# Zero products ahead of the first matmuls, and two of four modulation blocks multiplied in fp32 as they land

## The chip, the cores and the metric

The kernel runs on one core of one Trainium2 chip. The metric is the device time of one execution in microseconds. Three runs of the kernel before took 1945.74, 1946.46 and 1949.13 us (median 1946.46). TensorE multiplies (PE in the profile, its weight loads PEld), VectorE (DVE), ScalarE (ACT) and GpSimd (POOL) work on rows and columns, SyncE (SP) issues most DMAs.

## The reference

One layer of a diffusion backbone over 1024 latent and 256 context tokens of width 1024. What matters here is its start: a conditioning vector gives shift and scale of the first normalisation, and every projection reads the modulated tokens.

```
mod = (silu(cond) @ w_ada + b_ada)              # cond: two rows, c and c_ctx; w_ada: 1024 x 6144
sh1, sc1, gt1, sh2, sc2, gt2 = split(mod, 6)    # 1024 columns each
u = rmsnorm(x, g_norm1) * (1 + sc1) + sh1
proj = u @ w_in                                 # pooling, gating, q, k, v, output gate, branch gates
...                                             # three branches, merge, w_out, second norm, feed-forward
```

All inputs and outputs are fp32.

## The kernel before, in words

Tokens are in ten row tiles of 128 x 1024 (`xt[0]` to `xt[9]`; the first eight are latent). They are worked on in three groups of 512, 512 and 256 tokens. The projections need u transposed: per group g and k-tile k (128 of the 1024 columns), `tr(k, g)` (L251) makes up to four 128x128 transposes into one PSUM buffer (`pt_u` in the trace), and `mc(k, g)` (L255, through `modulate_cols`, L176) has ACT apply scale `a1` and shift `sh1` per column (`val_u`), stores the fp32 result to DRAM for later (`scr_u`, a POOL DMA), and has DVE split it into a rounded part and a rest (`u0h`, `u0l` and so on).

The number format matters. `F32R` is a reduced fp32 that PE multiplies in one pass. A product at nearly fp32 accuracy is made from three F32R products: high x high, high x low, low x high (`dense`, L117 to L125, three products of 128x512 for a k-tile of group 0). Weights are split the same way by `load_w` (L89): ACT copies to `hi`, DVE subtracts to `lo`.

Shift and scale come from the first 2048 columns of w_ada, in four blocks of 512 columns: blocks 0 and 1 are the two halves of the shift, 2 and 3 the two halves of the scale. Each block is eight landed tiles `ada[b, k]` of 128x512 fp32 (256 KB each, `wa` in the trace; L195 to L200 issue them on SP in the order 0, 2, weight k0, 1, 3). `mod_split(b, ks)` (L221) does, for each k-tile of a block:

- an ACT copy of the landed tile to F32R (`wah`) and a DVE subtract for the rest (`wal`);
- on PE, a product of `wah` with four columns, `shl`: the rounded cond of the two rows and what the rounding left; then, two tiles later, a product of `wal` with `sh0`: the rounded cond and two columns of zeros. Both go to one PSUM buffer `pm` (4 x 512).

`mod_cols(b)` (L235) turns the 4 x 512 row block into columns: an ACT copy out of PSUM (`mrow`), four pairs of tiny products of 4x128 by 4x2 (one for each 128 columns: `pmc`, eight records), a DVE add of the bias into `sh1` or `a1`, and for the scale a second DVE step with the norm's gain.

The order around the change is written out by hand. From L258 on, each engine handle is wrapped in `Pinned` (L35), which keeps that engine's instructions in program order until L412; what stands outside that stretch is ordered by the framework's own scheduler, and so are SP's DMAs. In the pinned stretch: row statistics of the first four x tiles (L259 to L261), `mod_split(0)`, `mod_split(2)` (L262, L263), the split of weight k0 (L264), three transposes, the first three tiles of block 1, `mod_cols(0)` and `mod_cols(2)` (L275, L276), then `mc(0)`, and a weave of the remaining tiles of blocks 1 and 3 with `tr`, `mc` and the `dense` products of k0 and v0 (L277 to L317). `mod_cols(1)` and `mod_cols(3)` come inside it, and `mc(4)` to `mc(7)` after them. Row statistics of the next four x tiles stand between (L302 to L319); then weight q0 is split (L320) and its products begin (L369).

Two DRAM-to-SBUF buffers (`raw`, NRAW = 2) hold landed weights; the fetch of q0 (L265) reuses k0's buffer and so waits until k0 is split. The big working tiles of 128x512 come from one pool of 59 slots (`slot`), PSUM from three buffers for sums (`ps_mm`) and five others (`ps_sd`).

In the trace nearly all instructions of the pinned stretch have line 43, the wrapper's; they are told apart by their tiles.

Of the kernel before, what the change touches and what calls it, by code (L numbers as in the profile page):

```python
# [7 lines left out]
F32 = mybir.dt.float32  # L8
# [6 lines left out]
P = 128  # L15
D = 1024
KT = D // P
# [31 lines left out]
def hybrid_step(  # L49
# [8 lines left out]
    V, A, G, PE = engines  # L58
    SP = nc.sync

    cp = ctx.enter_context(tc.tile_pool(name="cp", bufs=1))
# [7 lines left out]
    def slot(name, dt=F32R):  # L69
        return sp.tile([P, 512], dt, tag="s", name=name)  # L70
# [4 lines left out]
    def ps_mm(name):  # L75
        return pp.tile([P, 512], F32, tag="mm", name=name, bufs=3)

    def ps_sd(name):
        return pp.tile([P, 512], F32, tag="sd", name=name, bufs=5)
# [4 lines left out]
    def fetch_w(src, name):  # L84
        raw = wp.tile([P, 1024], F32, tag="raw", name=f"raw_{name}")
        SP.dma_start(raw, src)
        return raw

    def load_w(src, name, raw=None, eng=V):  # L89
        raw = fetch_w(src, name) if raw is None else raw  # L90
        hi = wp.tile([P, 1024], F32R, tag="hi", name=f"hi_{name}", bufs=NHL)
        lo = wp.tile([P, 1024], F32R, tag="lo", name=f"lo_{name}", bufs=NHL)
        A.copy(hi, raw)
        eng.tensor_tensor(lo, raw, hi.bitcast(F32), ALU.subtract)
        return hi, lo
# [21 lines left out]
    def dense(ps, w, acts, g, ks=range(KT)):  # L117
        n = GROUPS[g][1]
        whi, wlo = w
        for k in ks:  # L120
            ahi, alo = acts[k][g]
            s = slice(k * P, (k + 1) * P)
            PE.matmul(ps[:, :n], whi[:, s], ahi, start=k == 0, stop=False)
            PE.matmul(ps[:, :n], whi[:, s], alo, start=False, stop=False)
            PE.matmul(ps[:, :n], wlo[:, s], ahi, start=False, stop=k == KT - 1)  # L125
# [10 lines left out]
    ccol = cp.tile([P, NCOLS], F32, name="ccol")  # L136
    shl = cp.tile([P, KT, 4], F32R, name="shl")
    z = cp.tile([P, 10 * D], F32, name="z")
    cp.tile([P, 24], F32, name="pad1")
    cst = cp.tile([P, 3 * P + 2], F32, name="cst")  # L140
    SP.dma_start(ccol, cols)
    SP.dma_start(cst, consts)
# [27 lines left out]
    def transpose_cols(src, g, k, name):  # L170
        ps = ps_sd(f"pt_{name}{g}_{k}")
        for i in range(GROUPS[g][1] // P):
            PE.transpose(ps[:, i * P : (i + 1) * P], src[i][:, k * P : (k + 1) * P], ident)
        return ps

    def modulate_cols(dst, ps, g, k, a, sh, name):  # L176
        n, j = GROUPS[g][1], 1 if g == 2 else 0
        val = tmp(f"val_{name}{g}_{k}")
        A.activation(val[:, :n], ps[:, :n], AF.Identity, bias=sh[:, k, j : j + 1], scale=a[:, k, j : j + 1])
        if g < 2:  # L180
            nc.gpsimd.dma_start(scr_u[g][k], val)
        part = split_part(f"{name}{k}", g)
        put_split(part, val[:, :n])
        dst[k].append(part)
# [3 lines left out]
    def row_stats(i):  # L188
        row_rstd[i] = norm_rows(xt[i], 1, f"x{i}")

    def row_apply(i):
        V.tensor_scalar(xt[i], xt[i], row_rstd[i][:, 0:1], None, ALU.mult)

    ada = {}
    for b in (0, 2, 1, 3):  # L195
        if b == 1:
            raw_k0 = fetch_w(w_in[I_K], "k0")
# [5 lines left out]
        SP.dma_start(xt[i], xs[i])  # L203


    scond = cp.tile([P, KT, 2], F32, name="scond")
    cview = ccol[:, C_COND : C_COND + 16].rearrange("p (k j) -> p k j", j=2)
    A.activation(scond, cview, AF.Sigmoid)
    V.tensor_tensor(scond, scond, cview, ALU.mult)
# [9 lines left out]
    pms, los = {}, []  # L219

    def mod_split(b, ks=range(KT), behind=2):  # L221
        if b not in pms:
            pms[b] = ps_sd(f"pm{b}")
        pm = pms[b]
        for k in ks:
            wh, wl = slot(f"wah{b}_{k}"), slot(f"wal{b}_{k}")
            A.copy(wh, ada[b, k])
            V.tensor_tensor(wl, ada[b, k], wh.bitcast(F32), ALU.subtract)
            PE.matmul(pm[0:4, :], shl[:, k, :], wh, start=k == 0, stop=False)
            los.append((k, wl))  # L230
            while los and (k == KT - 1 or los[0][0] <= k - behind):
                k2, w2 = los.pop(0)
                PE.matmul(pm[0:4, :], sh0[:, k2, :], w2, start=False, stop=k2 == KT - 1)

    def mod_cols(b):  # L235
        half = b % 2
        kk = slice(half * 4, half * 4 + 4)
        mrow = mrows[half][0:4, (b // 2) * 512 : (b // 2 + 1) * 512]
        A.copy(mrow, pms[b][0:4, :])
        pmc = ps_mm(f"pmc{b}")  # L240
        pmv = pmc[:, 0:8].rearrange("p (c j) -> p c j", j=2)
        for c in range(4):
            PE.matmul(pmv[:, c, :], mrow[:, c * P : (c + 1) * P], cst[0:4, 3 * P : 3 * P + 2], start=True, stop=True)
        dst = sh1 if b < 2 else a1
        V.tensor_tensor(dst[:, kk, :], pmv, bav[:, b * 4 : b * 4 + 4, :], ALU.add)
        if b >= 2:
            V.scalar_tensor_tensor(a1[:, kk, :], a1[:, kk, :], 1.0, g1v[:, kk, :], ALU.add, ALU.mult)
# [3 lines left out]
    def tr(k, g=0):  # L251
        t0, n = GROUPS[g]
        u0[g, k] = transpose_cols(xt[t0 // P : (t0 + n) // P], g, k, "u")

    def mc(k, g=0):  # L255
        modulate_cols(uT, u0[g, k], g, k, a1, sh1, "u")

    V, A, G, PE = (Pinned(tc, e) for e in engines)  # L258
    for i in range(4):  # L259
        row_stats(i)  # L260
        row_apply(i)  # L261
    mod_split(0)  # L262
    mod_split(2)  # L263
    w_k0 = load_w(None, "k0", raw_k0)  # L264
    raw_q0 = fetch_w(w_in[I_Q], "q0")  # L265
    wg = [slot(f"wg{i}", F32).rearrange("p (k c) -> p k c", c=P) for i in range(2)]
    for i in range(2):
        SP.dma_start(wg[i], w_gate[:, 4 * i : 4 * i + 4, :])
    for i in (8, 9):
        SP.dma_start(xt[i], xs[i])  # L270
    tr(0)
    tr(1)
    tr(2)
    mod_split(1, (0, 1, 2))
    mod_cols(0)  # L275
    mod_cols(2)  # L276
    mod_split(1, (3,))  # L277
    mc(0)
    mod_split(1, (4,))
    mc(1)  # L280
    tr(3)
    ps_k0 = ps_mm("p_k00")
    dense(ps_k0, w_k0, uT, 0, (0,))
    mod_split(1, (5,))
    mc(2)
    tr(4)
    dense(ps_k0, w_k0, uT, 0, (1,))
    mod_split(1, (6, 7))
    mc(3)
    tr(5)  # L290
    dense(ps_k0, w_k0, uT, 0, (2,))
    mod_split(3, (0, 1))
    mod_cols(1)
    dense(ps_k0, w_k0, uT, 0, (3,))
    tr(6)
    mod_split(3, (2, 3))
    w_v0 = load_w(None, "v0", raw_v0)
    mod_split(3, (4, 5))
    ps_v0 = ps_mm("p_v00")
# [112 lines left out]
    V, A, G, PE = engines  # L412
# [84 lines left out]
    for g in range(3):  # L497
        t0, n = GROUPS[g]
# [526 lines left out]
    for ri, r in enumerate(ORDER):  # L1025
        scr = (scr_ya, scr_yb, scr_yc)[r]
        ys = [[] for _ in range(4)]
        for g in range(3):
            for kc in range(4):
                t0, n = GROUPS[g]  # L1030
# [6 lines left out]
        for d in range(KT):  # L1037
            if d % 2 == 0:
                wb = [load_half(w_branch[r, d // 2][:, i * 512 : i * 512 + 512], f"wb{r}_{d}_{i}") for i in range(2)]
            for g in range(3):  # L1040
                t0, n = GROUPS[g]
# [494 lines left out]
```

## Time and profile before

| what | value |
|---|---|
| median of three runs | 1946.46 us (1945.74 to 1949.13) |
| the profiled execution's own time | 1947.31 us |
| its span (first to last instruction) | 1945.5 us |
| DVE busy | 1294.0 us (67%) |
| ACT busy | 861.7 us (44%) |
| DMA, mean | 161 GB/s |
| first product of PE | at 11.88 us |

The chain of waits follows the work that ended last backwards from the end, and lists in order of time which wait or instruction was the last to hold it up. The timeline lists instructions with start and length, in microseconds; consecutive like ones are merged (x16 means sixteen), and a bracket gives the idle time before the instruction and what ended it. A matmul's length holds the pipe behind it (some 0.17 us), so PE's real step is the distance of two starts. The windows give busy times for a stretch, and the clock that was granted to TensorE as a share of full speed.

### The profile page before, as it was taken

The numbers are of one execution on the slowest core, as the hardware profiler recorded it, in microseconds if no ns is written. First come the engines' busy times: TensorE is split into PE (matmuls) and PEld (weight loads), VectorE is DVE, ScalarE is ACT, GpSimd is POOL, SyncE is SP. The second block draws the span as 40 slices with busy tenths as digits, with TensorE's granted clock in tenths as the row PEclk, the third lists the DMA queues.
The fourth block names the chain that finished last, engine by engine and source line by source line (L and its number), as shares of the span: only waits on it lengthen the run. The fifth ranks groups of instructions, "written<-read, shape, count | busy, mean of one in ns | idle before, by whom it ended". The sixth has DMA issues, their size and how long they took to land.

```text
span 1945.5 us, 28129 instructions
## 1 busy us (share of the span) xinstructions
PE 1903.0 (98%) x10136; PEld 1627.5 (84%) x10136; DVE 1294.0 (67%) x2207; ACT 861.7 (44%) x1768; POOL 378.2 (19%) x380
## 2 busy tenths in 40 slices
PE   6999999999999999999999999999999999999998
PEld 3778888998788888888888887888888888888886
DVE  6574443347759889875675599888776655744665
ACT  7444464653243333343123374555454545443443
POOL 1200001107302424220000015444431110000003
PEclk9999999999999999999999999999999999999999
DMA  9211111012635445469522435776773586654444
GB/s 361 85 59 33 43 39 40 27 56 70 203 119 165 149 158 164 153 211 321 163 97 98 152 120 212 253 264 246 259 269 136 193 333 203 210 170 151 165 133 159
DMA packets 149318, 313.32 MB, mean 161 GB/s; under 512 B 17550, under 2 KB 40818, under 8 KB 147130
## 3 DMA queue, kind: packets, MB, share of 16 engines
q1 hardware_dynamic: 107354, 220.73, 33.9%
q0 software_dynamic: 15520, 57.75, 7.8%
q10 hardware_dynamic: 26304, 33.04, 4.7%
q8 instruction: 79, 1.29, 0.3%
q14 instruction: 61, 0.50, 0.1%
HBM read 217.59 MB, written 93.36 MB: 160 GB/s over the span
## 4 chain that ended last, share of the span: by engine, by line
PE 87%; DVE 4%; DMA 3%; POOL 2%; ACT 1%; issue 1%; SPq 0%; POOLq 0%; ACTq 0%; DVEq 0%
PE w L1403 6%; PE w L1404 6%; PE w L1405 6%; PE pb L1050 3%; PE pb L1051 3%; PE pb L1052 3%; PE fT L892 3%; PE fT L890 3%; PE fT L891 3%; PE fB L891 2%; PE fB L890 2%; PE fB L892 2%; PE fT_g L892 2%; PE fT_g L890 2%; PE fT_g L891 2%; PE po L1168 2%
## 5 line engine op out<-in xcount | busy, mean ns | idle before, releaser
L1242 POOL TENSOR_TENSOR z<-z 128x512 f32<-128x512 f32 x64 | 100.1, 1564 | 123.3 <-DMA z<-in_w_ff 120.6
L947 DVE TENSOR_TENSOR z<-z 128x512 f32<-128x512 f32 x112 | 88.7, 792 | 2.5
L527 POOL PARTITION_ALL_REDUCE acc<-acc x16 | 54.6, 3446 | 184.0 <-DVE acc L521 113.6
L521 DVE SCALAR_TENSOR_TENSOR acc<-z,scond,acc 128x512 f32<-128x512 f32 x112 | 86.1, 816 | 0.0
L1357 POOL TENSOR_TENSOR rs_y<-rs_y,neghalf 128x1 f32<-128x1 f32 x10 | 9.6, 966 | 333.0 <-DVE rs_y L1356 333.0
L1208 ACT ACTIVATE z<-z 128x512 f32<-128x512 f32 x64 | 40.5, 632 | 69.8 <-DVE z L956 36.7
L972 ACT ACTIVATE z<-z 128x512 f32<-128x512 f32 x48 | 30.3, 632 | 59.1 <-DVE z L956 23.1
L130 POOL TENSOR_TENSOR rs_h<-rs_h,neghalf 128x4 f32<-128x4 f32 (+1 forms) x12 | 10.9, 910 | 200.5 <-DVE rs_h L129 200.3
L653 DVE SCALAR_TENSOR_TENSOR yc<-th,ccol,z 128x512 f32<-128x512 f32 (+1 forms) x12 | 7.9, 661 | 58.2 <-PE th L651 58.2
L1056 DVE TENSOR_TENSOR sg<-pb,sg 128x512 f32<-128x512 f32 (+1 forms) x48 | 28.7, 600 | 26.7 <-PE pb L1052 26.5
L881 ACT CAST hi_wb<-raw_wb 128x512 fp32r<-128x512 f32 x24 | 14.8, 620 | 64.4 <-PE pb L1051 37.6
L1209 ACT ACTIVATE z<-z 128x512 f32<-128x512 f32 x64 | 40.3, 629 | 1.1
L1171 DVE TENSOR_TENSOR po<-po,gt 128x512 f32<-128x512 f32 (+1 forms) x24 | 14.6, 607 | 35.1 <-PE po L1170 35.0
L1233 POOL DMA_DIRECT2D scr_s<-x x48 | 26.3, 549 | 53.1 <-DVE x L1227 47.6
L738 POOL TENSOR_TENSOR z<-z 128x1024 f32<-128x1024 f32 (+13 forms) x20 | 33.6, 1702 | 6.9 <-ACT z L722 4.6
L528 POOL TENSOR_TENSOR acc<-acc,bt 1x512 f32<-1x512 f32 x16 | 23.5, 1480 | 58.4 <-issue 58.4
L1174 ACT ACTIVATE po<-z 128x512 f32<-128x512 f32 (+1 forms) x24 | 12.7, 529 | 48.5 <-DVE z L1173 34.2
L587 DVE SCALAR_TENSOR_TENSOR z<-z,dmb,kv 128x129 f32<-128x129 f32 x56 | 16.6, 345 | 21.8 <-PE kv L576 21.3
L1057 DVE TENSOR_TENSOR z<-z,sg 128x512 f32<-128x512 f32 (+1 forms) x48 | 28.7, 601 | 1.2
L640 DVE TENSOR_TENSOR den<-den,gcol 128x2 f32<-128x2 f32 x40 | 6.2, 159 | 31.0 <-ACT den L639 29.9
L43 PE MATMUL pm<-wah,shl 128*4 128x512 f32 x32 | 13.8, 461 | 13.2 <-ACT wah L43 13.2
L130 POOL TENSOR_TENSOR rs_f<-rs_f,neghalf 128x4 f32<-128x4 f32 (+1 forms) x3 | 3.3, 1092 | 116.9 <-DVE rs_f L129 116.9
(5136 smaller groups left out, 7288.9 us busy)
## 6 DMA issues: line engine op xcount, KB each, us to landing
z<-in_w_ff SPq DMA_DIRECT2D x64, 512.0 KB, 5.5
z<-in_w_ada SPq DMA_DIRECT2D x64, 256.0 KB, 3.1
scr_t<-z POOLq DMA_DIRECT2D x16, 1024.0 KB, 4.9
z<-in_w_in SPq DMA_DIRECT2D x24, 512.0 KB, 4.3
scr_g<-z ACTq DMA_DIRECT2D x48, 256.0 KB, 2.0
sg<-scr_g SPq DMA_DIRECT2D x48, 256.0 KB, 4.5
scr_h<-z ACTq DMA_DIRECT2D x48, 256.0 KB, 3.6
scr_s<-x POOLq DMA_DIRECT2D x48, 256.0 KB, 4.3
```

What stands on the lines that cost most here:

```text
L521: V.scalar_tensor_tensor(acc[j], raw, scond[:, k, j : j + 1], acc[j], ALU.mult, ALU.add)
L890: PE.matmul(ps, whi[:, s], ahi, start=first and k == ks[0], stop=False)
L891: PE.matmul(ps, whi[:, s], alo, start=False, stop=False)
L892: PE.matmul(ps, wlo[:, s], ahi, start=False, stop=end and k == ks[-1])
L947: V.tensor_tensor(out, x, y, op)
L1050: PE.matmul(pb[:, :n], whi[:, s], yh, start=kc == 0, stop=False)
L1051: PE.matmul(pb[:, :n], whi[:, s], yl, start=False, stop=False)
L1052: PE.matmul(pb[:, :n], wlo[:, s], yh, start=False, stop=kc == 3)
L1242: G.tensor_tensor(out, x, y, ALU.subtract)
L1403: PE.matmul(banks[j], h_[:, s], rh, start=fp == 0, stop=False)
L1404: PE.matmul(banks[j], l_[:, s], rh, start=False, stop=False)
L1405: PE.matmul(banks[j], h_[:, s], rl, start=False, stop=fp == NFP - 1)
```

## The change

- `scond`, the two fp32 cond columns per k-tile, becomes part of a tile of four columns with zeros in the other two, so that it can be used directly as weights; a padding tile shrinks by the same 16 elements.
- A tile of zeros, `wt`, is written once, and `busy(30)` puts thirty F32R products of it by itself (128x128 by 128x512) at the head of PE's pinned order, into a PSUM buffer that nobody reads.
- `mod_direct(b, ks)` multiplies the landed fp32 tiles of a block by the fp32 cond columns: one fp32 product for each k-tile in place of two F32R products, one ACT copy and one DVE subtract. Blocks 0 and 1 (the shift) use it. Blocks 2 and 3 (the scale) keep `mod_split`.
- The order is rewritten: block 2's tiles are split in three portions with `mod_cols(0)`, `tr(0)` and `tr(1)` between, `mod_cols(2)` comes straight after `tr(1)`, the first three products of block 1 come after it, k0 is split after `mc(0)`, and the rest of block 1 is placed a little differently in the weave.

```diff
@@ -136,7 +136,7 @@
-    cp.tile([P, 24], F32, name="pad1")
+    cp.tile([P, 8], F32, name="pad1")
@@ -203,7 +203,9 @@
-    scond = cp.tile([P, KT, 2], F32, name="scond")
+    scond4 = cp.tile([P, KT, 4], F32, name="scond4")
+    scond = scond4[:, :, 0:2]
+    V.memset(scond4, 0.0)
@@ -232,6 +234,22 @@
+    def mod_direct(b, ks):
+
+        if b not in pms:
+            pms[b] = ps_sd(f"pm{b}")
+        for k in ks:
+            PE.matmul(pms[b][0:4, :], scond4[:, k, :], ada[b, k], start=k == 0, stop=k == KT - 1)
+
+    wt = slot("wt")
+    V.memset(wt.bitcast(F32), 0.0)
+    wps = ps_mm("warm")
+
+    def busy(n):
+
+        for _ in range(n):
+            PE.matmul(wps, wt[:, 0:P], wt, start=True, stop=True)
+
@@ -256,44 +274,46 @@
     V, A, G, PE = (Pinned(tc, e) for e in engines)
+    busy(30)
     for i in range(4):
         row_stats(i)
         row_apply(i)
-    mod_split(0)
-    mod_split(2)
-    w_k0 = load_w(None, "k0", raw_k0)
+    mod_direct(0, range(KT))
+    mod_split(2, (0, 1, 2, 3))
+    mod_cols(0)
+    mod_split(2, (4, 5))
+    tr(0)
+    mod_split(2, (6, 7))
+    tr(1)
+    mod_cols(2)
     raw_q0 = fetch_w(w_in[I_Q], "q0")
     wg = [slot(f"wg{i}", F32).rearrange("p (k c) -> p k c", c=P) for i in range(2)]
     for i in range(2):
         SP.dma_start(wg[i], w_gate[:, 4 * i : 4 * i + 4, :])
     for i in (8, 9):
         SP.dma_start(xt[i], xs[i])
-    tr(0)
-    tr(1)
+    mod_direct(1, (0, 1, 2))
     tr(2)
-    mod_split(1, (0, 1, 2))
-    mod_cols(0)
-    mod_cols(2)
-    mod_split(1, (3,))
     mc(0)
-    mod_split(1, (4,))
+    w_k0 = load_w(None, "k0", raw_k0)
     mc(1)
     tr(3)
     ps_k0 = ps_mm("p_k00")
     dense(ps_k0, w_k0, uT, 0, (0,))
-    mod_split(1, (5,))
+    mod_direct(1, (3, 4))
     mc(2)
     tr(4)
     dense(ps_k0, w_k0, uT, 0, (1,))
-    mod_split(1, (6, 7))
+    mod_direct(1, (5,))
     mc(3)
+    mod_direct(1, (6, 7))
     tr(5)
+    mod_split(3, (0, 1))
     dense(ps_k0, w_k0, uT, 0, (2,))
-    mod_split(3, (0, 1))
     mod_cols(1)
+    mod_split(3, (2, 3))
     dense(ps_k0, w_k0, uT, 0, (3,))
     tr(6)
-    mod_split(3, (2, 3))
     w_v0 = load_w(None, "v0", raw_v0)
     mod_split(3, (4, 5))
     ps_v0 = ps_mm("p_v00")
```

## The prediction, made before the changed kernel was run

> **What bounds the kernel now.** I read the page first, then the chain of waits of the first 60 us, then the timeline there, then the windows.
>
> ```profile
> span 1945.5 us, 28129 instructions
> PE 1903.0 (98%) x10136; PEld 1627.5 (84%) x10136; DVE 1294.0 (67%) x2207; ACT 861.7 (44%) x1768; POOL 378.2 (19%) x380
> ```
>
> PE is busy 98% of the span, so what it idles at the head is most of what it idles at all. The change touches only instructions before 46 us. The chain of waits (start, us, what) says what that stretch hangs on:
>
> ```profile
> 7.38 6.67 DMA wa<-in_w_ada
> ...
> 25.02 4.53 DMA wa<-in_w_ada
> ...
> 37.97 0.70 PE p_k L43 x3
> ...
> 39.14 0.98 PE pmc L43 x8
> ...
> 41.02 0.44 PE pt_u L43 x4
> ...
> 44.66 1.40 PE pm L43 x6
> 46.09 0.58 ACT mrow_lo L43
> ...
> 56.09 1.15 DVE lo_q L94
> 57.23 0.04 issue
> 57.28 2.55 PE p_q L43 x10
> ```
>
> Three stages: until about 30 us the w_ada blocks arriving; from 30 to 46 us PE; from 46 to 57 us ACT and DVE (modulated columns, row statistics); then PE again. These rows also give PE's steps at full clock: 0.70 us for the three products of a k-tile of a dense group, 0.98 for the eight small products of mod_cols, 0.44 for the four transposes of tr. The timeline shows what the first stage waits for inside:
>
> ```profile
> 11.23 10.01 ACT L43 CAST wah<-wa 128x512 fp32r<-128x512 f32 x16
> ...
> 14.09 9.71 DVE L43 TENSOR_TENSOR wal<-wa,wah 128x512 fp32r<-128x512 f32 x16
> ...
> 17.78 0.63 PE L43 MATMUL pm<-wah,shl 128*4 128x512 f32 x1
> ...
> 18.20 0.63 PE L43 MATMUL pm<-wal,sh 128*4 128x512 f32 x1
> ...
> 20.53 0.40 PE L43 MATMUL pm<-wah,shl 128*4 128x512 f32 x1
> ...
> 20.76 0.39 PE L43 MATMUL pm<-wal,sh 128*4 128x512 f32 x1
> ...
> 21.80 1.05 ACT L43 CAST hi_k<-raw_k 128x1024 fp32r<-128x1024 f32 x1 [0.56 <-DMA raw_k<-in_w_in]
> ...
> 23.86 0.40 PE L43 MATMUL pm<-wal,sh 128*4 128x512 f32 x1 [0.20 <-DVE wal L43]
> ...
> 24.34 1.05 ACT L43 COPY mrow_hi<-pm 4x512 f32<-4x512 f32 x2
> ...
> 26.43 1.94 PE L43 MATMUL pmc<-cst,mrow_hi 4*128 4x2 f32 x16
> ...
> 28.61 0.17 DVE L43 SCALAR_TENSOR_TENSOR a<-a,ccol 128x8 f32<-128x8 f32 x1
> ...
> 28.87 0.78 ACT L43 ACTIVATE val_u<-pt_u,sh,a 128x512 f32<-128x512 f32 x1 [2.96 <-DVE a L43]
> ```
>
> ACT casts sixteen tiles without a break (10.01/16 = 0.63 us each), DVE subtracts sixteen (9.71/16 = 0.61 each) and is the last, at 23.8. Only then come the copies, the small products and a1, and mc(0) starts at 28.87. Consecutive starts show PE's step for 128x512 in fp32r: 0.42 us at 17.8, 0.23 at 20.5. That is a clock that changes, and the windows show when (columns: length, PE, PEld, DVE, ACT, POOL busy, granted clock, DMA share, GB/s):
>
> ```profile
> 22.13:25.55 3.42, 3.00 (x19) 1.80 (x19) 3.42 (x6) 3.42 (x7) 0.00 (x0) 1.00 1.05 401
> 25.55:28.96 3.41, 3.38 (x23) 2.12 (x20) 1.88 (x6) 0.45 (x2) 0.00 (x0) 1.00 1.06 407
> 28.96:32.37 3.41, 2.16 (x8) 1.57 (x9) 3.04 (x6) 3.41 (x6) 1.44 (x3) 0.50 1.05 413
> 32.37:35.79 3.42, 3.42 (x12) 2.33 (x11) 3.35 (x8) 2.39 (x5) 1.03 (x2) 0.50 1.03 419
> ...
> 1158.76:1162.18 3.42, 2.98 (x13) 2.63 (x14) 2.12 (x8) 3.42 (x9) 0.00 (x0) 0.50 0.62 223
> 1162.18:1165.59 3.41, 3.41 (x30) 3.41 (x31) 3.41 (x12) 2.55 (x6) 1.22 (x1) 1.00 0.40 161
> ```
>
> I cut them at the places where the clock changes: steps of 3.41 us. From 28.96 to 35.79 PE runs at half clock, after a window that held mostly the sixteen small products; a window that PE fills ends it. (Before 18.7 us nothing is recorded and the column shows 1.00; the 0.42 us step shows half.) The DMAs run at 400 GB/s throughout, so a 256 KB tile takes 0.65 us, and k0 (512 KB, behind the 16 tiles of blocks 0 and 2) landed at 21.8. Counted back: the last tile of block 2 at 20.5, of block 0 at 15.3, the first of block 0 at 10.7. Forward: blocks 1 and 3 are complete at 32.2. The change moves none of these DMAs.
>
> **The change, part by part.** *Zeros.* A memset without inputs goes to the front of DVE's queue:
>
> ```profile
> 0.84 0.09 DVE L211 MEMSET sh<- 128x32 f32 x1
> ```
>
> So the products start at about 1.5 us. The first whole window ends 3.4 to 6.8 us later; until then 8 to 16 products take 0.42 us, the others 0.23: 8.4 to 9.9 us together. They end at 9.9 to 11.4, when the first tile lands (10.7). Cost: at most 0.7 us, on a block that has slack.
>
> *Block 0 in fp32.* No row shows fp32 products with four weight columns. The nearest are pool_out's, 128x512 fp32:
>
> ```profile
> 489.30 2.31 PE L763 MATMUL pp<-xp,z 128*128 128x512 f32 x6
> ...
> 490.15 0.19 PEld L763 LDWEIGHTS pp<-xp,z 128*128 128x128 f32 x1 [0.24 <-issue]
> 490.58 0.19 PEld L763 LDWEIGHTS pp<-xp,z 128*128 128x128 f32 x1 [0.24 <-issue]
> ```
>
> Two records for each product, 0.43 us apart: 0.855 us, against 0.46 for the pair that it replaces. The lower bound is the pair's own 0.46, the upper 1.71 (half clock); I take 0.855, since a pair's weight columns do not show in its step either (0.23 for 4 columns, 0.70/3 for 128). Eight take 6.84 us: 10.7 to 17.5 (18.2 if the zeros end late).
>
> *Block 2 first at the casts.* ACT's queue is now free, so casts follow landings: tile 3 lands at 17.9, is cast by 18.55; the copy of block 0's row (0.58) ends at 19.2, eight small products at 20.2, sh1 at 20.45. DVE has the subtracts of tiles 4 to 7 behind sh1: 4 x 0.61, to 22.9. PE's last product ends at 23.15, the copy starts 0.25 later. From a copy's start to a1 the trace of block 3 shows 46.09 to 48.00 + 0.17:
>
> ```profile
> 47.80 0.17 DVE L43 TENSOR_TENSOR a<-pmc,ccol 128x8 f32<-128x8 f32 x1 [2.47 <-PE pmc L43]
> 48.00 0.17 DVE L43 SCALAR_TENSOR_TENSOR a<-a,ccol 128x8 f32<-128x8 f32 x1
> ```
>
> So a1 is ready at 23.4 + 2.1 = 25.5, and mc(0) starts at 25.6: **3.25 us earlier**.
>
> *Block 1 in fp32, from 25.1 us (end of the small products) to the end of block 3's products.* PE's work: 8 x 0.855 = 6.84; 16 products of block 3 x 0.23 = 3.7; six dense k-tiles x 0.70 = 4.2; tr(2) to tr(6) 5 x 0.44 = 2.2; mod_cols(1) 1.0: 17.9 us, ending at 43.0. Before, the same place is 46.06 less 0.2 us of pipe: 45.9, after 17.5 us from 28.4. In these 17.5 the work was 12 products of block 1 (2.8) + 3.7 + 4.2 + four tr 1.8 + 1.0 = 13.5; the other 4 were half clock and the wait for the cast that ended at 30.16. So the lost clock comes back (4), and fp32 takes it again (6.84 - 2.8 = 4.0, and one tr 0.44). What remains is the earlier start: **2.9 us**. Nothing else binds: ACT and DVE lose eight casts and subtracts here, k0's lo is ready at 28.7 where PE asks at 28.9, tiles of block 3 land 8 us before use. load_w of k0 moves behind mc(0), so its buffer is free at 28.7, not 25; q0's fetch, which waits for that buffer, was issued at 35.8 behind other DMAs, so this costs nothing. The cover gone, q0 would be late by as much.
>
> *After 43 us* the order is as before: ACT and DVE from the row copy to lo_q, then PE. x rows 4 to 7 land by about 40 (four times 1.3 us, and the writes of u, behind v0), before ACT asks for them. So 57.28 becomes 54.4, and the rest shifts.
>
> Sum: -2.9 + up to 0.2 for late zeros = -2.8 us. The profiled execution took 1947.31 (span 1945.5 and 1.8 around it), 0.85 over the median of the runs, 1946.46. Span 1942.7, and on the median 1946.46 - 2.8 = **1943.7**.
>
> **The rivals.** About 0.2% (3.9 us) is what a measurement of this kernel can tell from no change; the gain lies under it.
>
> *Zeros do not release the clock* (slower). No row shows a product of zeros. If the gate looks at data, the thirty take 30 x 0.43 = 12.8 us, to 14.3, and block 0 starts at half clock: 1.71 each for 3.4 to 6.8 us, the rest 0.855, ending at 22.9 to 24.1. Behind it stand 16 products 3.7, mod_cols(0) 1.0, two tr 0.9 and 2.4 to a1: mc(0) at 30.9 to 32.1, 2 to 3.2 us late. 1946.46 + 2.6 = 1949.1. It decides once block 0 ends after 20 us. For it: only that data is unknown; against: the page's clock follows how full the windows are.
>
> *A second loss of the clock* behind the sparse stretch from 22 to 25 us (waiting for DVE, copy, small products): one window at half costs 3.4 x 0.5 = 1.7 us, giving 1945.4. The window 25.55 to 28.96 that lost the clock held, beside the sixteen small products, five or six of 0.23 (1.2 us, a third). The emptiest window that I can lay over my own order, 21.7 to 25.1, still holds 1.25 us of products and the 0.44 of tr(1), half. The Trainium skill (TensorE: Matmul & The Clock Gate, "Why this matters for your kernels") asks only for no idle gap over about 3 us. By that rule this rival would be nil, but the clock went at 28.96 after a window counted 3.38 us busy: the trace disagrees. The same page (Part 4, PE-mode transpose) says that transposes do not count as busy. By it, that window would be a third full as well, and the loss likely.
>
> ```profile
> 1159.12 2.39 PE L1142 MATMUL pt<-cst,xn 128*128 128x128 f32 x10 [3.03 <-ACT xn L1134]
> ```
>
> Here the window 1158.76 to 1162.18, filled by ten transposes, brought the clock back, so they count, and the rival stays small.
>
> *Late zeros*: the memset behind the cond columns, at 3.8 us; block 0 then ends at 19.3 to 20, a1 1.4 to 2 us later: 1945.3.
>
> *Later clock losses fall otherwise.* PE idles 3.62 us here (and 3.03 in the row above):
>
> ```profile
> 134.29 1.97 PE L478 MATMUL pc<-cst,z 36*128 36x36 f32 x20 [3.62 <-DVE z L466]
> ```
>
> Each was followed by half clock. Windows cut elsewhere through such gaps can halve or avoid it: 1.7 us or more off, 1942.0 to 1940.5.
>
> **How the numbers follow.** Main case 0.57 (1942.4 to 1945.0: one k-tile step either way in the DVE chain, and the zeros); later losses avoided 0.19; second loss 0.09; late zeros 0.08; zeros not counted 0.07. Range: 1940.8 to 1946.9, which leaves out most of the last case and the ends. Faster by over 0.2% (below 1942.6): the avoided losses and the main case's lower edge, 0.33. Slower by over 0.2%: half of the zeros case and a little for an order that changes downstream, 0.05. Within: 0.62.
>
> **What would show it.** Right: zeros from about 1.5 us, a step of 0.23 by 8 us; fp32 products of block 0 as two records 0.43 apart, ending near 17.5; mc(0) near 25.6; clock 1.00 from 25 to 45 us; block 3's last product near 43; lo_q's products near 54.4. Wrong: a step of 0.42 in all thirty zeros; fp32 products slower than 0.855; a clock of 0.50 between 20 and 45 us; mc(0) later than 27; a later stage whose length differs.

## The result and the profile after

The changed kernel is slower: a median of 1954.1 us over 20 runs, against 1948.71 us for the kernel before over 20 runs. The ratio is 1.0028, with a 95% interval of 1.0020 to 1.0035: 4 to 7 us more, where 2.8 us less was forecast. One of the 20 runs of the changed kernel, 2118.13 us at a granted clock of 0.849, is slow and left out of the ratio. The forecast of 1943.7 stood on the median of three runs, 1946.46; over 20 runs the kernel before is 2.25 us higher. The profiled execution took 1952.96 us, its span is 1951.1.

The chain of waits of the changed kernel, first 62 us (start, us, what):

```profile
2.50 6.22 DMA sel<-in_sel
8.74 0.17 DVE selr L525
8.91 0.05 issue
8.96 0.48 DVE wt L245
9.45 0.04 DVE s_x L43
9.50 9.16 PE warm L43 x30
18.66 8.45 PE pm L43 x22
27.11 0.98 PE pmc L43 x8
...
31.19 0.58 ACT mrow_hi L43
...
32.87 2.67 PE pm L43 x6
35.53 1.02 PE pt_u L43 x8
...
37.26 1.81 PE pm L43 x4
39.07 0.59 PE pt_u L43 x4
...
47.47 0.44 PE pt_u L43 x4
...
50.19 1.40 PE pm L43 x6
...
61.62 1.15 DVE lo_q L94
```

Read it from the top. The kernel before waited for w_ada; now the head hangs on a 3 KB transfer, `sel`, that has nothing to do with the modulation. VectorE casts it (`selr`), and behind that cast, next in VectorE's order, stands the memset of the zero tile:

```profile
6.39 0.14 DVE L475 COPY mprev<-m0t 4x1 f32<-4x1 f32 x1
8.74 0.17 DVE L525 CAST selr<-sel 100x8 fp32r<-100x8 f32 x1 [2.21 <-DMA sel<-in_sel]
8.96 0.48 DVE L245 MEMSET wt<- 128x512 f32 x1
```

It runs at 8.96 us, not at 1. The zeros then occupy TensorE from 9.50 to 18.66, and everything in its queue comes after: block 0 ends near 25.4 where 17.5 was forecast, and the chain stays on PE. The two places that the prediction names are in the timeline (start, length, engine, line, operation):

```profile
18.59 7.03 PE L43 MATMUL pm<-wa,scond 128*4 128x512 f32 x16
...
33.36 0.78 ACT L43 ACTIVATE val_u<-pt_u,sh,a 128x512 f32<-128x512 f32 x1 [1.60 <-DVE a L43]
...
61.53 1.22 DVE L94 TENSOR_TENSOR lo_q<-raw_q,hi_q 128x1024 fp32r<-128x1024 f32 x1
```

mc(0) starts 4.5 us later than before (28.87), not 3.25 earlier, and lo_q's subtract 5.53 us later (56.00 before), and the spans differ by about as much: 1951.1 - 1945.5 = 5.6. That these two agree is partly chance. In between the lag is not constant: the first product of `pb` is 8.66 us late (868.65 against 859.99), and about 3 us are regained between 1170 and 1300 us. Some of this is scatter between executions (see the kernel before, profiled once more); the rest was not tried. The windows at the steps of the clock (length, PE, PEld, DVE, ACT, POOL busy, granted clock, DMA share, GB/s):

```profile
10.49:13.90 3.41, 3.41 (x9) 2.64 (x8) 2.02 (x7) 1.08 (x4) 1.09 (x2) 1.00 1.05 402
13.90:17.31 3.41, 3.41 (x16) 2.80 (x15) 2.20 (x6) 1.27 (x3) 0.55 (x1) 1.00 1.05 405
...
30.97:34.38 3.41, 3.18 (x17) 1.67 (x16) 0.54 (x3) 1.59 (x3) 0.00 (x0) 1.00 1.03 420
```

Eight zero products start in the first window and fifteen in the second: the distance of two starts falls from 0.43 to 0.23 us, so the clock doubles at 13.90 us, under products of zeros alone. From there to beyond 45 us it stays whole.

### The profile page after: what moved, and what is told of

The parts are those of the page before. It is cut to its first block, busy times and chain, and to the rows that moved or that the text cites. A ratio compares the mean times of both kernels' runs of the same rounds, so it can differ in the third digit from the quotient of the medians.

```text
span 1951.1 us, 28133 instructions
## 1 busy us (share of the span) xinstructions
PE 1913.3 (98%) x10166; PEld 1632.3 (84%) x10166; DVE 1287.0 (66%) x2193; ACT 852.3 (44%) x1752; POOL 381.4 (20%) x380
## 4 chain that ended last, share of the span: by engine, by line
PE 87%; DVE 7%; issue 2%; ACT 2%; POOL 1%; DMA 1%; POOLq 0%; DVEq 0%; ACTq 0%; SPq 0%
PE w L1423 6%; PE w L1424 6%; PE w L1425 6%; PE fT L912 3%; PE fT L910 3%; PE fT L911 3%; PE pb L1071 3%; PE pb L1070 3%; PE pb L1072 3%; PE fB L912 2%; PE fB L910 2%; PE fB L911 2%; PE po L1188 2%; PE po L1189 2%; PE po L1190 2%
## 5 line engine op out<-in xcount | busy, mean ns | idle before, releaser
L967 DVE TENSOR_TENSOR z<-z 128x512 f32<-128x512 f32 x112 | 94.5, 844 | 2.5
L1074 DVE TENSOR_TENSOR z<-pb,sg 128x512 f32<-128x512 f32 (+1 forms) x24 | 14.2, 599 | 18.6 <-PE pb L1072 18.5
```

The lines of the kernel that those rows point to most:

```text
L967: V.tensor_tensor(out, x, y, op)
```

## The experiments

**Early zeros: only the zero tile and its memset are moved up.**

```diff
     V.memset(neghalf, -0.5)
+    wt = slot("wt")
+    V.memset(wt.bitcast(F32), 0.0)
...
-    wt = slot("wt")
-    V.memset(wt.bitcast(F32), 0.0)
```

> The changed kernel with the memset of the zero tile moved up beside the first memset of the program, so that it no longer stands in VectorE's queue behind the cast that waits for the sel DMA (landed at 8.7 us). Nothing else is changed. Theory A (the whole loss is the late start of the zeros, which pushes TensorE's queue by some 8 us): zeros from about 1.3 us instead of 9.50, end before 11.5, block 0 done near 17.6 instead of 25.4, mc(0) near 25.7 instead of 33.36, last product of block 3 near 43.8 instead of 51.4; total 7 to 8 us below the changed kernel, that is 1 to 3 us below the kernel before. Theory B (the fp32 products of block 1 in the stretch that TensorE bounds are the loss): mc(0) is early, but block 3's last product is no earlier than before (45.9) and the total is no better than the kernel before.

Median 1948.74 us over 12 runs; against the kernel before 0.9996 (0.9986 to 1.0006). By the medians that is 5.4 us below the changed kernel, where 7 to 8 were expected, and no loss is left against the kernel before. The timeline:

```profile
0.93 0.48 DVE L148 MEMSET wt<- 128x512 f32 x1
...
1.47 8.46 PE L43 MATMUL warm<-wt 128*128 128x512 f32 x30 [1.47 <-DVE mprev L466]
...
11.02 7.03 PE L43 MATMUL pm<-wa,scond 128*4 128x512 f32 x16 [1.08 <-DVE s_x L43]
...
25.78 0.78 ACT L43 ACTIVATE val_u<-pt_u,sh,a 128x512 f32<-128x512 f32 x1 [1.60 <-DVE a L43]
...
53.96 1.22 DVE L94 TENSOR_TENSOR lo_q<-raw_q,hi_q 128x1024 fp32r<-128x1024 f32 x1
```

Zeros at 1.47 us, ended at 9.9, block 0 at 11.0, mc(0) at 25.78 (the prediction had 25.6), lo_q 7.57 us earlier than in the changed kernel and 2.04 earlier than in the profile of before. Theory A holds for the cause of the loss. The gain against the kernel before, expected at 1 to 3 us, is not shown: the medians differ by 0.8 us, and the interval includes no change.

**No zeros.** `busy(30)` and its tile are taken out; the rest of the change stays.

> The changed kernel without the zero tile and its thirty products. Theory A: block 0 starts when its first tile lands (about 10.8 us) at half clock, 1.71 us for a product until a 3.41 us window is full, and ends at 19.3 to 20.6; mc(0) at 27 to 28.3, total 4.5 to 6 us below the changed kernel, within 1.5 us of the kernel before: the zeros as they were placed cost more than they gave. Theory B: still 3 us or more slower than the kernel before. If zeros that start early are worth anything, this is 1.4 to 2.7 us slower than the kernel with early zeros.

1951.85 us; 1.0012 (1.0001 to 1.0023). That is 2.3 us above the kernel before beside it, where at most 1.5 was expected. mc(0) at 27.87, as expected, and lo_q at 55.98, within 0.02 us of the profile of before. At lo_q, late zeros are worse than none by 5.55 us (61.53 against 55.98), and early zeros are worth 2.0 us (55.98 against 53.96), the half clock that block 0 otherwise runs at:

```profile
11.04 9.09 PE L43 MATMUL pm<-wa,scond 128*4 128x512 f32 x16 [11.04 <-DVE s_x L43]
```

9.09 us for the eight products that took 7.03 behind the zeros.

**Zeros on the kernel before.** The early memset and thirty products, nothing else of the change.

> The kernel before with the early zero tile and thirty zero products at TensorE's head, nothing else of the change. Theory A: casts and landings bound the head of the kernel before, so a released clock there brings nothing: zeros end near 10 us, the clock falls back before 19 us because the few products of block 0 leave windows half empty, mc(0) stays at 28.9, total within 1 us of the kernel before. Rival (the gain of the released clock is what counts, not the fp32 products): 1.5 us or more faster than the kernel before.

1949.1 us; 0.9996 (0.9984 to 1.0007). mc(0) at 28.88, as expected; lo_q at 54.83. The clock came at 5.93 us and was not lost until 29.83, for one window of 3.41 us, so that detail of the expectation was wrong. The total shows no difference.

**Block 1 split again, with early zeros.** `mod_direct(1, ...)` becomes `mod_split(1, ...)` at all its places.

> Early zeros, block 0 in fp32, but block 1 cast and split as before, in the places where the change multiplies it in fp32. Theory A (worked out by the rows): TensorE saves 3 us of products, but ScalarE and VectorE get eight casts and subtracts back, and TensorE waits for them; mc(0) near 25.9, block 3's last product 44.7 or later, about 1 to 2 us slower than the kernel with early zeros and within 1 us of the kernel before. Theory B (fp32 in block 1 is what costs): 2 to 3 us faster than the kernel with early zeros.

1950.25 us; 1.0006 (0.9996 to 1.0016). lo_q at 54.85, 0.9 us later than with block 1 in fp32. TensorE now waits for VectorE between 26 and 45 us (engine, what, for whom: total us, times, longest):

```profile
PE pm L43 <- DVE wal L43: 1.9, 4, 1.3
PE p_k L43 <- DVE lo_k L94: 0.6, 1, 0.6
PE p_k L43 <- DVE u0h L43: 0.4, 1, 0.4
PE p_k L43 <- DVE u0l L43: 0.2, 1, 0.2
```

With block 1 in fp32 the same view has no wait at all from 26 to 44. The seven waits come to 3.1 us, and each record also holds some 0.17 us of pipe, in which no product starts. TensorE so loses more than it saves in products: its last product of block 3 starts at 44.50 us, against 43.61 with block 1 in fp32. Theory B falls.

**Sixty early zeros instead of thirty.**

> Early zeros, but sixty products instead of thirty. Theory A: TensorE works them off in order before block 0, thirty more at 0.23 us are 6.8 us, less the 1.1 us that TensorE waited for the first tile: zeros end near 16.8, block 0 5.8 us later than with thirty, mc(0) near 31.5, total 5 to 6 us above the kernel with thirty early zeros, which is what the late memset costs the changed kernel. Theory B (the late memset itself, through VectorE's and ScalarE's queues, is what costs): no more than 1 us slower than with thirty.

1952.72 us; 1.0014 (1.0004 to 1.0025). The timeline:

```profile
1.48 15.57 PE L43 MATMUL warm<-wt 128*128 128x512 f32 x60 [1.48 <-DVE mprev L466]
...
16.98 7.03 PE L43 MATMUL pm<-wa,scond 128*4 128x512 f32 x16
...
31.75 0.78 ACT L43 ACTIVATE val_u<-pt_u,sh,a 128x512 f32<-128x512 f32 x1 [1.60 <-DVE a L43]
```

Block 0 starts 5.96 us later, mc(0) 5.97, lo_q 5.97 (59.93): a delay of TensorE's queue at the head arrives whole at 60 us. Here the memset stands early, so TensorE's lost time alone is enough for a loss of the size of the change's. The medians differ by 4.0 us, in two sets of runs, where 5 to 6 were expected.

**Twelve late zeros.** The changed kernel, with `busy(12)`.

> The changed kernel with its late memset, but twelve products instead of thirty. Theory A: zeros from 9.5 to 13.5 or 14.6 (half clock until a 3.41 us window is full), block 0 ends near 21, mc(0) at 28.5 to 29.6, total about 4 us below the changed kernel and 1 to 2 us above the kernel before. Theory B: as slow as the changed kernel, since the memset stands where it stood.

1950.14 us; 1.0000 (0.9989 to 1.0011). Zeros from 9.06 to 14.4, mc(0) at 29.21, lo_q at 57.38, 4.15 us earlier than with thirty. Of this 0.44 is the memset, which ran at 8.52 us here instead of 8.96; the rest is the fewer products behind a late memset. 4 us come off the median, as expected, but against the kernel before there is no difference, where 1 to 2 us were expected.

**The kernel before, profiled once more.**

> The kernel before, unchanged, profiled once more. Between 555 and 860 us every profile of a kernel made here, even of one whose instructions there are in the same order as in the kernel before, lost 2.2 to 3.5 us on the first profile of the kernel before. If that is scatter from execution to execution, this profile differs from the first one there by the same amount, with the head (mc(0) at 28.9, lo_q's subtract at 55 to 56) as before. If it comes from the early products, this one is like the first.

One run, 1946.97 us, span 1945.2. Its head is not that of the first profile: lo_q starts at 54.46, not 56.00. From its timeline, and two of its windows:

```profile
24.26 1.47 PE L43 MATMUL pt_u<-cst,z 128*128 128x128 f32 x12
25.49 0.93 PE L43 MATMUL pm<-wah,shl 128*4 128x512 f32 x3
26.26 0.40 PE L43 MATMUL pm<-wal,sh 128*4 128x512 f32 x1
26.58 1.94 PE L43 MATMUL pmc<-cst,mrow_hi 4*128 4x2 f32 x16
...
54.46 1.22 DVE L94 TENSOR_TENSOR lo_q<-raw_q,hi_q 128x1024 fp32r<-128x1024 f32 x1
```

```profile
24.77:28.18 3.41, 3.41 (x28) 2.63 (x26) 2.31 (x5) 1.14 (x3) 0.00 (x0) 1.00 1.06 402
28.18:31.59 3.41, 2.13 (x14) 1.30 (x14) 2.66 (x7) 2.56 (x5) 0.93 (x2) 1.00 1.06 410
```

Here the clock came at 17.94 us instead of 18.72, so the windows cut the sparse stretch from 25.5 to 30.4 in two, and the clock was not lost. And between 555 and 860 us this profile loses 2.3 us of its lead of 2.9, with the same program: the first product of `pb` is at 859.3, against 860.0. Every other profile here loses 2.2 to 3.7 us on the first one in this stretch, so the 2.3 of it are scatter from execution to execution, and not the change's.

**A version that beats both.** Early zeros; the last two k-tiles of block 1 split instead of multiplied in fp32; and sh1's add held back until block 2's small products are done.

```diff
+        if b == 0:
+            held[0] = pmv
+            return
+        if b == 2:
+            V.tensor_tensor(sh1[:, 0:4, :], held[0], bav[:, 0:4, :], ALU.add)
...
-    mod_direct(1, (6, 7))
+    mod_split(1, (6, 7))
```

> Early zeros, and two more steps taken off the path that the trace with early zeros shows: the add of sh1 is held back until the small products of block 2 are done, so that VectorE's subtracts of block 2 no longer stand behind it, and the last two k-tiles of block 1 are cast and split instead of multiplied in fp32 (ScalarE and VectorE have the time by then). Theory A (TensorE's queue from the zeros to block 3 is the path, term by term): mc(0) 0.3 us earlier than with early zeros (25.5), block 3's last product another 0.8 us earlier, lo_q's subtract near 52.9 instead of 53.96; total 2 to 4 us below the kernel before. Theory B (nothing is left to gain at the head): no earlier than with early zeros.

1946.17 us over 12 runs; 0.9980 (0.9969 to 0.9990), against 1950.3 for the kernel before beside it. lo_q is 0.77 us earlier than with early zeros:

```profile
53.19 1.22 DVE L94 TENSOR_TENSOR lo_q<-raw_q,hi_q 128x1024 fp32r<-128x1024 f32 x1
```

mc(0) was not earlier (25.84, with block 0's first product 0.26 us later), so the held add is not shown to be worth anything. From mc(0) to the last product of block 3 it is 17.00 us instead of 17.83, which fits the two k-tiles; the two steps were not tried apart. The medians differ by 4.1 us, more than the head explains (2.81 us at lo_q against the first profile of before, 1.27 against the second); the medians of the kernel before in the sets of runs here differ by 1.6 us among themselves (1948.71 to 1950.3).

## Why the prediction was wrong

**The step that failed** is the first of the sum: "A memset without inputs goes to the front of DVE's queue." It rested on one row, the memset of `sh0`, and on an instruction that the framework's scheduler is free to place. It placed this one twelfth, behind a cast that waits for a DMA. Moving two lines of text moved it. So the zeros began 8 us late, and thirty products of no use, worked off before block 0, delay everything behind them. The sum has at most 0.2 us for late zeros; they cost 7.57 us at lo_q (61.53 against 53.96). The mechanism stood among the rivals, late zeros, but with a start of 3.8 us and a price of 1.6, since only the cond columns were looked at as something to wait for. The profile of before had a larger bound, a cast of VectorE that needs a DMA and stands outside the pinned stretch:

```profile
10.83 0.17 DVE L505 CAST selr<-sel 100x8 fp32r<-100x8 f32 x1
```

Why the scheduler chose that place was not tried.

**Zeros and the clock: right.** They release it, in the changed kernel after one window that they fill, with early zeros after one that they fill for 2.95 of its 3.41 us. The rival in which they do not falls.

**fp32 products with four weight columns: right, 0.43 us a record** (7.03 us for sixteen, less 0.17 of pipe), the same as pool_out's with 128 columns.

**TensorE's 17.9 us after the small products: too small by 0.75.** The rows of the chain above show where: three fp32 products take 2.67, not 2.57 (twice), two take 1.81, not 1.71, and transposes behind fp32 products take 1.02 for eight and 0.59 for four (at 39 and again at 43 us), not 0.88 and 0.44. In the row at 47.47, behind fp32r products, they take 0.44. Going into a run of fp32 products costs 0.10 us, and coming out of one into transposes 0.14 to 0.15; no row that the prediction shows has that. With it the forecast of 2.8 becomes 2.05; the kernel with early zeros gave 2.04 at lo_q, against the same first profile of before.

**"The lost clock comes back (4)": right for that one execution only.** The second profile of before does not lose it, and is 1.5 us faster at the head. A gain that is counted against one profile's clock phase need not be there in the median; against this second profile, the changed kernel with early zeros is only 0.5 us earlier at lo_q. So even with the zeros in time, the forecast 2.8 us would not have come; the medians show 0.8.

**DVE's queue behind sh1, the landings, the stage from 46 to 57 us: right.** mc(0) came within 0.2 us with the memset moved up, and the later stages shifted as a whole.

**A second loss of the clock between 20 and 45 us** did not happen in any of the kernels with the new order that were profiled. The later losses did not fall away: in the changed kernel half clock stood for 6.83 us from 140.2 and for 3.4 us from 1167.6, as long as before. With early zeros, but also in the second profile of before, the first of them took 3.41 us, so this too varies from execution to execution.

## What to carry to other kernels

Filler ahead of real work in an engine's order is safe only if its inputs are certain to be ready first: look up the built order of the engine that makes them, and what each instruction ahead waits for. Count the end of a clock loss as a gain only if the loss shows in more than one execution. And price a product in another format with the changes of format around it.

## What the runs showed of the hardware

- Products of zeros alone release the clock: it doubled at 13.90 us in the changed kernel, and at 4.4 us with early zeros, 2.9 us after the first of them.
- The busy time that the profile counts does not tell whether a window loses the clock. In the first profile of before, 25.55 to 28.96 counted 3.38 us busy, with about 1.2 us of products beside the small ones, and lost it. In the second, 24.77 to 28.18 held four 0.23 us products, 0.7 us of transposes and the small products, and kept it, and so did 28.18 to 31.59, which counted only 2.13 us busy. Products and transposes fill about 1.6 and 1.7 us of these two, so in these windows it went with them; where the limit lies is not measured.
- An fp32 product of 128x512 takes 0.855 us at full clock whether it has 4 weight columns or 128. Going into a run of them costs 0.10 us (2.67 us for three, 1.81 for two), and transposes behind one cost 0.14 to 0.15 us more than behind fp32r products.
